# One more slot between the transposes of the values and those of the scaled key in each head pair's chain

## The chip, the cores and the metric

The kernel runs on one core of a Trainium2 chip. The metric is device time in microseconds (us) of one execution. Five engines work side by side, each through its own list of instructions and in the order of that list: PE (matmuls), DVE and ACT (elementwise work), POOL (elementwise work and the issue of some DMAs) and SP (the issue of the other DMAs). An engine whose next instruction waits, waits with everything that stands behind it.

## The reference

One layer of a hybrid encoder is computed for 1024 prompt frames and 64 sample frames, in fp32. A normalised input goes through one projection of 2560 columns, which are split among three token mixers; their outputs are normalised, joined, projected and added to the input, and a feed-forward part follows:

```python
proj = einsum('bld,de->ble', rmsnorm(x), w_in)
q, f_raw, inp, g, u, xr, gr = split(proj)
oA = hgrn2(q, f_raw, inp, g)   # 6 heads of 64: S = diag(f) S + k i^T, o = S^T q, norm, silu(g)
oB = s5(u)                     # 16 complex diagonal systems, 64 states each
oC = rglru(xr, gr)             # conv of width 4, two gates, h = a h + b, gelu(gr)
x = x + concat(oA, oB, oC) @ w_out
y = rmsnorm(x + (silu(rms(x) @ w_gate) * (rms(x) @ w_up)) @ w_down)
```

## The kernel before

The tokens are cut into three groups of 384, 384 and 320 (`GROUPS`). The first part of the program, some 550 us, holds the input projections, the three mixers and the output projection; the rest is the feed-forward part, which the change does not touch.

**Slots.** The input projection is done 128 columns at a time: `proj` issues 24 matmuls into one of two PSUM buffers of the tag "mm" and loads its two weight blocks, raw by SP, high part by ACT (L117), low part by ACT and a POOL DMA (L119, L120). After each projection `drive` calls `tick`, which lets every chain that is due take one step. One projection and the steps behind it are a *slot* here. PE takes its instructions strictly in the order in which the program issues them; DVE, ACT, POOL and SP are ordered by a scheduler by readiness and priority.

**Chains.** The 384 columns of a mixer are three head pairs. For each pair `inproj` does six projections in a row: xr, f, q, v, gr, g, each evacuated by DVE (L411, L425, L432, L437, L443, L453), which frees its "mm" buffer. With xr the chain `unit` of this pair starts, so there are nine chains, six slots apart, and one that lasts 15 slots overlaps the next two. A chain yields the number of slots to its next step: convolution (L490 to L492) at 0; the two gate matmuls (wab, wxb) at 2; logarithms (L511 to L521) at 3; exponentials at 4; the scaled queries and keys q32, Q2, k32, kh at 5; ks, in the tag "la" (L583 to L585), at 6; at 7 the transposes of v (`turned`, L604). Then come three steps which are each one slot behind the one before: kt, the transposes of ks, with the masked score matmuls (L618 to L658, called *masked* below); the state products kv and the state updates (L661 to L684); the output product po and its evacuation by ACT L696 and DVE L697. The square sums (sqn) follow two slots later.

**Shared storage.** All matmul results but the projections' share a ring of six PSUM banks, the tag "mx": masked takes four, the transposes and each gate one. The tag "d16" holds in turn l2 (L510, L512), d16, and the copy of kt; "la" holds the gate's la (L503) and then ks. There is one g per head pair in one buffer: L453 writes it, L697 reads it.

**The S5 mixer** has its own chain, which takes part in the same slots: scar/sbbr and scai/sbbi products, evacuated by ACT L899 and DVE L902 and written out by DMAs of SP (L909); transposes of sbv and sH, copied by DVE L888 into sMV; products with sMT, sMV and sX. After the last chain has started, `outproj(0)` does the output projection of the first group, with split operands mh (ACT L160) and ml (DVE L167).

Of the kernel before, what the change touches and what calls it, by code (L numbers as in the profile page):

```python
# [58 lines left out]
def trunk(ctx: ExitStack, tc: tile.TileContext, I: dict, O: list):  # L59
# [214 lines left out]
    with ExitStack() as ph1:  # L274
# [114 lines left out]
        def inproj(gi):  # L389
# [10 lines left out]
            for p in range(3):  # L400
                o = proj(gi, 1792 + 128 * p)
                with tc.high_priority(offset=WPRIO):
                    xr = tile_("xr", TMAX + 6)
                    off = 0
                    for s0, n, kind in grp["segs"]:
# [12 lines left out]
                        off += n + 3  # L418
                u = dict(xr=xr)
                spawn(unit(gi, p, u))  # L420
                yield
                o = proj(gi, 384 + 128 * p)
# [51 lines left out]
        def unit(gi, p, u):  # L474
# [116 lines left out]
            def turned(src, name, cp):  # L591
                dst = p1.tile([128, 3, 128], F32, tag=name, name="turned")
                pt = ps_mx()
                ptv = pt[:, :384].rearrange("p (c w) -> p c w", c=3)
                for c in range(ncp):
                    transpose(ptv[:tw[c], c, :], src(c), ident)
                nf = sum(1 for w in tw if w == 128)
                with soon():
                    cp(dst[:, :nf, :], ptv[:, :nf, :])
                    if nf < ncp:  # L600
                        cp(dst[:64, nf, :], ptv[:64, nf, :])
                return dst

            vt = turned(lambda c: u["v"][:, 128 * c:128 * c + tw[c]], "vt", A.copy)  # L604
            if p == 2:
# [8 lines left out]
                        stt(o, o, hc[:, 9 + j:10 + j], lsq[:, :T], op0=OP.mult, op1=OP.mult)  # L614

                pending.append((lsq[:, :T], 1.0 / (4 * DC), lru_done))
            yield 1
            kt = turned(lambda c: ks[:, 128 * c:128 * c + tw[c]], "d16", A.copy)  # L618
            a = am
            nf = sum(1 for w in tw if w == 128)  # L620
# [819 lines left out]
```

## Time and profile before

| what | value |
|---|---|
| time, median of 3 runs | 1385.76 us (1381.37 to 1386.45) |
| profiled execution | 1382.6 us, its span 1380.8 us |
| mean granted TensorE clock | 0.961 |
| PE busy | 1306.4 us, 95% of the span |
| DVE, ACT, POOL busy | 622.2, 634.5, 292.1 us |

The times of rows are counted from the start of the span. PE bounds the kernel as a whole; its idle time and its slower stretches lie almost wholly in the first 550 us, where DVE, ACT and SP each hold it up now and then.

### The profile page before, as it was taken

How to read it: one execution, taken by the hardware profiler on the slowest of the kernel's cores; microseconds unless marked ns; L12 is line 12 of the kernel's file. 1: busy time of each engine (PE TensorE's matmuls, PEld its weight loads, DVE VectorE, ACT ScalarE, POOL GpSimd, SP SyncE). 2: the span in 40 equal slices, each digit the busy share in tenths (PEclk: the TensorE clock that was granted, in tenths of full speed). 3: DMA queues.
4: the chain of work that ended last, by engine and by line, in shares of the span. 5: the costliest groups of instructions: out<-in, count | busy, mean ns of one | idle time of the engine just before them, and what ended most of it. 6: DMA issues, size and time to landing. Idle time of an engine off the chain costs nothing.

```text
span 1380.8 us, 21166 instructions
## 1 busy us (share of the span) xinstructions
PE 1306.4 (95%) x7872; PEld 1254.1 (91%) x7872; DVE 622.2 (45%) x1714; ACT 634.5 (46%) x1244; POOL 292.1 (21%) x359
## 2 busy tenths in 40 slices
PE   7886999999998999999999999999999999999995
PEld 6776798878887798999999999999999999999985
DVE  8884798857856677821121111221112111211287
ACT  7667566768976454542322332222321233222363
POOL 2233353444432000111122010220111111110000
PEclk8997899999988899999999999999999999999997
DMA  9967677768775245444355252553454335432343
GB/s 281 273 145 183 131 168 155 169 150 178 167 164 143 81 138 161 115 90 94 63 99 114 65 118 50 96 122 69 92 107 92 77 74 119 90 82 64 86 133 118
DMA packets 106119, 169.81 MB, mean 123 GB/s; under 512 B 12849, under 2 KB 35905, under 8 KB 106017
## 3 DMA queue, kind: packets, MB, share of 16 engines
q0 software_dynamic: 35936, 62.30, 28.2%
q1 hardware_dynamic: 70080, 106.16, 25.0%
q8 instruction: 62, 1.02, 0.3%
q14 instruction: 41, 0.33, 0.1%
HBM read 160.71 MB, written 7.12 MB: 122 GB/s over the span
## 4 chain that ended last, share of the span: by engine, by line
PE 51%; issue 25%; DVE 10%; POOL 6%; DMA 4%; ACT 3%; SPq 1%; POOLq 0%; DVEq 0%; ACTq 0%
PE pd L76 16%; PE pu L76 10%; PE pg L76 10%; PE mm L76 9%; PE mx L76 5%; POOL wlo L120 4%; DMA wlo<-in_w_in_dram 2%; DMA wlo<-in_w_up_dram 1%; ACT wlo L119 1%; ACT L138 1%; DMA xraw<-in_xT_dram 0%; ACT whi L117 0%; DMA raw<-in_w_in_dram 0%; DVE xl L328 0%; SPq L909 0%
## 5 line engine op out<-in xcount | busy, mean ns | idle before, releaser
L117 ACT CAST whi<-raw 128x512 fp32r<-128x512 f32 x320 | 190.2, 600 | 255.4 <-PE pd L76 175.3
L1332 DVE TENSOR_TENSOR sil<-pu,sil 128x384 f32<-128x384 f32 (+1 forms) x66 | 35.4, 536 | 398.9 <-PE pu L76 398.9
L76 PE MATMUL mm<-xh,whi 128*128 128x384 f32 (+1 forms) x480 | 170.0, 363 | 19.6 <-ACT whi L117 11.6
L76 PE MATMUL pd<-hh,whi 128*128 128x384 f32 (+1 forms) x528 | 172.2, 330 | 0.0
L76 PE MATMUL pd<-hl,whi 128*128 128x384 f32 (+1 forms) x528 | 171.5, 329 | 0.0
L76 PE MATMUL pg<-x2h,whi 128*128 128x384 f32 (+1 forms) x528 | 170.3, 327 | 0.6 <-ACT x2h L261 0.6
L76 PE MATMUL pg<-x2l,whi 128*128 128x384 f32 (+1 forms) x528 | 170.4, 327 | 0.3 <-DVE x2l L262 0.3
L76 PE MATMUL pu<-x2h,whi 128*128 128x384 f32 (+1 forms) x528 | 170.0, 326 | 0.0
L76 PE MATMUL pu<-x2l,whi 128*128 128x384 f32 (+1 forms) x528 | 169.9, 326 | 0.0
L76 PE MATMUL mm<-xl,whi 128*128 128x384 f32 (+1 forms) x480 | 158.4, 340 | 0.0
L119 ACT ACTIVATE wlo<-whi 128x512 fp32r<-128x512 f32 x248 | 145.1, 606 | 3.9 <-PE mm L76 0.9
L120 POOL DMA_DIRECT2D wlo<-in_w_in_dram x112 | 99.7, 974 | 215.3 <-ACT wlo L119 179.8
L1342 DVE TENSOR_TENSOR x<-pd,x 128x384 f32<-128x384 f32 (+1 forms) x120 | 64.3, 536 | 166.4 <-PE pd L76 166.2
L120 POOL DMA_DIRECT2D wlo<-in_w_gate_dram x44 | 42.6, 968 | 440.2 <-ACT wlo L119 433.8
L76 PEld LDWEIGHTS mm<-xh,whi 128*128 128x128 f32 x480 | 96.1, 202 | 28.2 <-ACT whi L117 13.3
L1333 ACT CAST hh<-sil 128x384 fp32r<-128x384 f32 (+1 forms) x66 | 32.7, 496 | 185.9 <-DVE sil L1332 185.9
L76 PE MATMUL pd<-hh,wlo 128*128 128x384 f32 (+1 forms) x528 | 107.5, 329 | 0.0
L76 PE MATMUL mm<-xh,wlo 128*128 128x384 f32 (+1 forms) x480 | 92.3, 332 | 9.3 <-DMA wlo<-in_w_in_dram 9.2
L76 PEld LDWEIGHTS pd<-hl,whi 128*128 128x128 f32 x528 | 100.3, 190 | 0.0
L76 PEld LDWEIGHTS pd<-hh,whi 128*128 128x128 f32 x528 | 100.2, 190 | 0.0
L76 PEld LDWEIGHTS pg<-x2l,whi 128*128 128x128 f32 x528 | 99.1, 188 | 1.0 <-DVE x2l L262 0.7
L76 PEld LDWEIGHTS pg<-x2h,whi 128*128 128x128 f32 x528 | 99.1, 188 | 0.9 <-ACT x2h L261 0.9
(428 smaller groups left out, 2525.8 us busy)
## 6 DMA issues: line engine op xcount, KB each, us to landing
raw<-in_w_in_dram SPq DMA_DIRECT2D x112, 256.0 KB, 4.5
wlo<-in_w_in_dram POOLq DMA_DIRECT2D x112, 256.0 KB, 5.9
raw<-in_w_down_dram SPq DMA_DIRECT2D x56, 256.0 KB, 2.7
raw<-in_w_out_dram SPq DMA_DIRECT2D x48, 256.0 KB, 3.0
raw<-in_w_gate_dram SPq DMA_DIRECT2D x44, 256.0 KB, 2.9
raw<-in_w_up_dram SPq DMA_DIRECT2D x44, 256.0 KB, 5.5
wlo<-in_w_gate_dram POOLq DMA_DIRECT2D x44, 256.0 KB, 4.7
wlo<-in_w_up_dram POOLq DMA_DIRECT2D x44, 256.0 KB, 6.6
```

The costliest lines, as they stand in the source:

```text
L76: in_order(PE.matmul(out, lhsT, rhs, start=start, stop=stop, **kw).ins)
L117: ins = A.copy(hi[:, :n, :], raw[:, :n, :]).ins
L119: A.activation(lo[:, :n, :], hi[:, :n, :].bitcast(F32), AF.Copy, scale=-1.0)
L120: G.dma_start(lo[:, :n, :], src[:, h0:h0 + n, :], accum_op=OP.add)
L138: ins = A.activation(out, in_, func, **kw).ins
L1332: tt(s_[:, :T], pu[:, :T], s_[:, :T], op=OP.mult)
L1333: A.copy(hh[:, t0:t0 + T], s_[:, :T])
L1342: tt(x1[gi][:, dm, :T], o[:, :T], x1[gi][:, dm, :T], op=OP.add)
```

## The change

One number: the chain waits two slots, not one, behind the transposes of v. kt with masked, kv, po and sqn come a slot later in each of the nine chains, and with them the chain's end. No instruction is added or taken away on any engine's arithmetic.

```diff
@@ unit(gi, p, u)
                 pending.append((lsq[:, :T], 1.0 / (4 * DC), lru_done))
-            yield 1
+            yield 2
             kt = turned(lambda c: ks[:, 128 * c:128 * c + tw[c]], "d16", A.copy)
```

On PE the first place is the slot at 154 us of the trace before, where the second chain is at its kt and the third at its gates. Before:

```order
L79 MATMUL mx<-ident,sbv 128x128 x2
L79 MATMUL mx<-ident,sH_1744 128x128 x2
L79 MATMUL mx<-ident,la 128x128 x3
L76 MATMUL mx<-qm,km 128x128 x6
...
L76 MATMUL mx<-xc,wab 128x384
L76 MATMUL mx<-xc,wxb 128x384
L76 MATMUL mm<-xh_342,whi 128x384
```

Now, with the projection of 24 matmuls and the S5 products in between left out:

```order
L79 MATMUL mx<-ident,sbv 128x128 x2
L79 MATMUL mx<-ident,sH_1741 128x128 x2
L76 MATMUL mx<-xc,wab 128x384
L76 MATMUL mx<-xc,wxb 128x384
L76 MATMUL mm<-xh_342,whi 128x384
...
L79 MATMUL mx<-ident,la 128x128 x3
L76 MATMUL mx<-qm,km 128x128 x6
```

The gates of the younger chain stay in their slot and go on right behind the transposes of S5; kt (ident,la) and masked (from qm,km on) stand behind the next projection.

On DVE the second place is the end of the third chain, at 230 to 237 us before: L697 is its output, L453 the g of the fourth chain. Before:

```order
L697 SCALAR_TENSOR_TENSOR mix0_714<-mx_2518,hc_493,g_2172 128x384 [waits Activation_49]
L614 SCALAR_TENSOR_TENSOR mix0_714<-mix0_714,hc_493,lsq_501 128x384 [waits Activation_49]
L614 SCALAR_TENSOR_TENSOR mix0_714<-mix0_714,hc_493,lsq_501 128x384 x2
L566 TENSOR_TENSOR dd_2748<-eb_2666 128x6x2 [waits Activation_49]
L569 TENSOR_TENSOR q32_2749<-q_2403,eb_2666 128x192
L567 TENSOR_TENSOR dd_2748<-dd_2748 128x6 [waits DVE_49]
L572 TENSOR_TENSOR Q2_2750<-q32_2749,eb_2666 128x6x2x16 [waits DVE_49]
L453 TENSOR_TENSOR g_2719<-mm_2694,rt1_92 128x384 [waits PE_49]
```

Now:

```order
L614 SCALAR_TENSOR_TENSOR mix0_714<-mix0_714,hc_493,lsq_501 128x384 [waits Activation_49]
L941 TENSOR_TENSOR sbv_2711<-st1_2603,mx_2714 128x2x137 [waits DVE_49]
L942 TENSOR_TENSOR sXb_2712<-st2_2604,mx_2713 128x2x137
L697 SCALAR_TENSOR_TENSOR mix0_714<-mx_2629,hc_493,g_2157 128x384 [waits Activation_49]
L943 TENSOR_TENSOR sX1_2710<-sbv_2711,sXb_2712 128x2x137 [waits DVE_49]
L453 TENSOR_TENSOR g_2704<-mm_2679,rt1_92 128x384 [waits DVE_49]
L614 SCALAR_TENSOR_TENSOR mix0_714<-mix0_714,hc_493,lsq_501 128x384 x2
```

L453 stands nearly at once behind L697, with a wait for DVE's own L697 in place of one for PE, since the old g is read a slot later than the new one is projected; the six instructions that stood between them come later.

## Rows read from the trace of the kernel before

**Rows 1.** Busy time by stretch: the densest of the mixers, and the feed-forward part.

```profile
core 0: us, PE busy (x) PEld busy (x) DVE busy (x) ACT busy (x) POOL busy (x), PEclk, DMA share, GB/s
180.00:240.00 60.00, 57.02 (x366) 51.63 (x363) 54.84 (x141) 37.79 (x77) 28.81 (x32) 0.97 0.78 165
540.00:1380.00 840.00, 820.38 (x4960) 815.62 (x4958) 221.88 (x483) 274.13 (x519) 117.22 (x136) 0.99 0.43 94
```

**Rows 2.** Waits of PE from 60 to 550 us: total, times, longest.

```profile
PE mm L76 <- DVE g L453: 4.1, 2, 3.0
```

**Rows 3.** Timeline of PE: start, length, instruction; the slot at 154, one like it.

```profile
154.21 0.49 PE L79 MATMUL mx<-ident,la 128*128 128x128 f32 x3
...
160.17 0.69 PE L76 MATMUL mx<-q,k 64*128 64x64 f32 x2 [3.32 <-DVE sMV L888]
...
171.13 0.39 PE L76 MATMUL mx<-scar,sbbr 64*16 64x128 f32 x2
...
204.33 0.49 PE L79 MATMUL mx<-ident,la 128*128 128x128 f32 x3
...
213.42 0.38 PE L79 MATMUL mx<-ident,sbv 128*128 128x128 f32 x2
```

**Rows 4.** Timeline of PE, two projections from 233 us, and two like them.

```profile
233.13 0.81 PE L76 MATMUL mx<-sqn,ones_h 128*128 128x384 f32 x2
236.91 0.69 PE L76 MATMUL mm<-xh,whi 128*128 128x384 f32 x1 [2.98 <-DVE g L453]
...
247.56 0.39 PE L76 MATMUL mx<-sU,sMT 128*128 128x137 f32 x2
...
280.71 0.91 PE L76 MATMUL mx<-sqn,ones_h 128*128 128x384 f32 x2
...
290.14 0.49 PE L79 MATMUL mx<-ident,la 128*128 128x128 f32 x3
```

**Rows 5.** Timeline of PE, the last products of two chains' po.

```profile
181.01 0.66 PE L76 MATMUL mx<-Q,hist 128*128 128x64 f32 x4
...
222.92 0.66 PE L76 MATMUL mx<-Q,hist 128*128 128x64 f32 x4
```

**Rows 6.** Timeline of DVE at the same two chains' ends.

```profile
186.23 0.60 DVE L697 SCALAR_TENSOR_TENSOR mix<-mx,hc,g 128x384 f32<-128x384 f32 x1
...
230.50 0.61 DVE L697 SCALAR_TENSOR_TENSOR mix<-mx,hc,g 128x384 f32<-128x384 f32 x1
231.03 3.23 DVE L614 SCALAR_TENSOR_TENSOR mix<-mix,hc,lsq 128x384 f32<-128x384 f32 x3
...
236.31 0.55 DVE L453 TENSOR_TENSOR g<-mm,rt 128x384 f32<-128x384 f32 x1
```

**Rows 7.** Timeline of PE behind the slot at 290 us.

```profile
295.20 1.65 PE L76 MATMUL mx<-xc,wab 128*128 128x384 f32 x2 [1.48 <-ACT turned L599]
298.58 1.65 PE L76 MATMUL mx<-xc,wxb 128*128 128x384 f32 x2 [1.73 <-ACT turned L599]
...
304.83 0.40 PE L76 MATMUL mx<-sU,sMT 128*128 128x137 f32 x2
```

**Rows 8.** Timeline of PE in the slot at 418 us.

```profile
418.33 0.52 PE L79 MATMUL mx<-ident,la 128*128 128x128 f32 x3 [2.64 <-DVE la L584]
...
427.34 1.41 PE L76 MATMUL mx<-xc,wab 128*128 128x320 f32 x2 [2.06 <-DVE xc L492]
...
433.91 0.93 PE L76 MATMUL mx<-turned 64*128 64x128 f32 x10
```

**Rows 9.** Timeline of PE at its longest wait.

```profile
95.14 1.04 PE L76 MATMUL mx<-qm,km 64*128 64x128 f32 x10
...
98.24 0.39 PE L76 MATMUL mx<-scar,sbbr 64*16 64x128 f32 x2
...
110.65 0.69 PE L76 MATMUL mm<-xh,whi 128*128 128x384 f32 x1 [9.43 <-ACT whi L117]
```

**Rows 10.** Waits of SP from 60 to 550 us.

```profile
SPq L909 <- DVE sysb L902: 22.7, 4, 11.3
```

**Rows 11.** Timeline of PE at the start of the output projection.

```profile
452.80 3.50 PE L76 MATMUL mm<-ml,whi 128*128 128x384 f32 x7 [2.58 <-DVE ml L167]
```

## The prediction

> **What bounds the kernel now.** I read the busy times by stretch first. In the feed-forward part PE is busy 820.4 of 840 us at a granted clock of 0.99 [rows 1]; the change moves nothing there. In the mixers PE still has the longest list, but DVE is nearly as full: between 180 and 240 us it is busy 54.8 of 60 us, PE 57.0 [rows 1]. So a wait of PE that is removed there is a gain only as far as DVE can follow; its 5.2 idle us in that stretch are the room. Second, the waits of PE and its timeline before 550 us. The reader is to see few and single waits with different causes, and that each costs more than its length, because the matmuls behind it run at the lower of the two clock levels (1.2 instead of 2.4 GHz) for a while. So each place is priced by comparing it with the same instructions elsewhere at full clock.
>
> **The change part by part.** Work is not added; kt, masked, kv, po and sqn of nine chains go one projection later. That costs or gains only where PE waits now, or would wait then.
>
> *The slot at 154 us.* kt to the start of the next slot's work takes 171.13 − 154.21 = 16.9 us; the same instructions, kt, masked, gates and a projection, take 213.42 − 204.33 = 9.1 us [rows 3]. So the place costs 7.8 us, 3.3 of them a wait and 4.5 slow clock. The wait is that of masked for a bank of the ring: DVE has copied sMV too late (L888). S5's two transposes, kt, four banks of masked and the gates, nine uses of six banks, fall into one slot. With the change masked stands behind the gates and a projection, some 6 us later on PE, and the copies' 3.3 us of lateness are covered. The DVE queue that made them late does not get shorter; it will then hold up a projection's buffer or a gate instead. Bounds 0 and −7.8; I take half, **−4**.
>
> *Two projections from 233 us.* sqn to the end of two projections takes 247.56 − 233.13 = 14.4 us, elsewhere 290.14 − 280.71 = 9.4 [rows 4]: 5.0 us lost, 3.0 of them a wait for DVE's L453, which must free the "mm" buffer. L453 comes at 236.31 although its product was long done: 3.2 us of L614, L566 and others stand between L697 and L453 [rows 6]. In the new order L453 is second behind L697, with most of these behind it. L697 itself waits for po, a slot later, but DVE reached it at 230.50, 6.9 us after po's last product ended (222.92 + 0.66) [rows 5, 6], so po can end one projection later, 4.3 us ((9.4 − 0.8) / 2, [rows 4]), before DVE notices. L453 would then come some 1.2 us behind L697, near 232, before the buffer is due at 233.9. Bounds +1 and −5.0; I take **−4**.
>
> *The slot at 290 us.* From kt at 290.14 to 304.83 are 14.7 us [rows 4, 7] against 9.1 [rows 3]: 5.6 lost. The gates wait for ACT's copy of kt, which stands in ACT's queue behind a weight block's high part; this came late because SP's queue had been held by L909. That wait, SP for L902, is the largest that S5 gives the DMA queue: four times, 22.7 us in all, 11.3 the longest [rows 10]. The gates no longer stand behind kt, but the next projection needs that same late weight block, and PE reaches it 3.6 us earlier, since kt and masked now come behind it. I expect most of the wait to move to the projection. Bounds +2 and −5.6; I take **−1.5**.
>
> *The first chain, 95 to 110 us.* This is the same cause before its longest wait, 9.4 us for a high part [rows 9]. Today masked, 98.24 − 95.14 = 3.1 us, and kt, 0.5, come ahead of the S5 products that start L902's chain; now these run 3.6 us sooner, and SP is released up to that much sooner, but 3.6 us of PE work move from ahead of the wait to behind it. The two cancel, except that a queue passes on less than it is given. Bounds 0 and +3.6; I take **+1**.
>
> *The slot at 418 us.* From the end of a projection at 418.33 − 2.64 = 415.69 to 433.91 pass 18.2 us, for work that takes at most 9.1 [rows 8, 3]. kt waits 2.64 us for L584, then the gates 2.06 us for the convolution, L492, whose steps on DVE were interleaved with masked's evacuation. Now kt has a slot's cover and its wait goes; but the gates come straight behind the projection, where the convolution is not ready either. The two waits and the 7 us of slow kt and masked between them end at 427.34; without masked's evacuations in between, the convolution should be done about 5.5 us behind the projection, so one wait of about 5.5 us takes the place of two of 4.7. What is won is some slow clock: bounds +2 and −9.1; nearest is the wait that stays, so **−2**.
>
> *The start of the output projection.* The first ml (L167) is 2.6 us late and is followed by seven matmuls in 3.5 us, about twice the length at full clock [rows 11]. The last chains are a slot longer now, so DVE has more of them at this time, and ml stands in the same queue. Bounds 0 and +6; I take **+2**.
>
> *The new wait.* L453 of chains 2 to 9 waits for L697, so for po in the same slot. Behind po lies one projection, 4.3 us, until the buffer is due; L696, L697 and L453 need about 1.6 (L697 and L453 0.6 each [rows 6], L696 taken as the same). So it waits only if DVE is more than 2.7 us behind. At 186 us DVE is 4.6 us behind po (186.23 − 181.67), at 230 us 6.9 [rows 5, 6]. Because po itself comes later while DVE's backlog does not, most of that is used up. Bounds 0 and +10; I take **+1**. Nothing but the DVE instructions behind L453 is queued behind this wait, and these serve the next chain's steps.
>
> *What DVE gives back.* 8 us are to be gained at 154 and 233 us, both around a stretch with 5.2 us of DVE idle. I charge **+2** (bounds 0 and +5).
>
> Sum: −4 − 4 − 1.5 + 1 − 2 + 2 + 1 + 2 = **−5.5 us**. The profiled execution took 1382.6 us, 1.8 of them outside its span of 1380.8; 5.5 less gives 1377.1. The median of the runs, 1385.76, lies 3.2 above the profiled one, so a median would be 1380.3. I forecast **1380 us**.
>
> The Trainium skill, in "TensorE: Matmul & The Clock Gate", section "A second HAM failure mode: psum-queue depth-cycling", says that short idle moments of PE between groups of matmuls, while results cycle through PSUM banks, can make its clock fall and rise again and again. The rows agree in kind: 3.3 us of wait at 160.17 go with 4.5 us of slow matmuls [rows 3]. By that rule a change that replaces one long wait with several short ones would gain nothing, and the sum by it would be about 0; without the rule the sum stays −5.5.
>
> **The rivals.** *Nothing to measure.* All gains are taken back: DVE and SP release the same buffers at the same times, and PE only waits elsewhere. For it speaks DVE's 54.8 of 60 us [rows 1] and that two of the five places hang on SP and the weight blocks, not on the order of PE. Against it: at 154 us the banks, not the queue, were short. It gives −2 to +2, so about 1386 on the median.
>
> *Slower, by the buffers of the projections.* L453 behind L697 holds one of only two "mm" buffers through po, L696 and L697 at eight places, from the slot of the second chain's g on. If DVE's backlog is as far behind the later po as it was behind the earlier, the projection two slots on waits 4.6 − 2.7 = 1.9 us at the place of 186 us and 6.9 − 2.7 = 4.2 us at that of 230 us [rows 5, 6], each with slow matmuls behind, as long again by [rows 3]: some 12 us. With what is won at 154 us it gives +8, 1394 on the median. The point from which it decides: L697 starting more than 2.7 us behind po's last product. Against it: today PE waits only twice for L453, 4.1 us in all [rows 2], though the same queue stands ahead of it.
> The Trainium skill ("Perfetto Trace Analysis", section "Optimization Strategy") reads a gap that repeats on the engine that should be busy as a sign that too few buffers are there for the next tile. Today's rows show two such waits of nine [rows 2], so they do not bear it out yet; with it, all eight places would repeat the gap.
>
> *All of it.* The places at 154, 233 and 290 us lose their full 7.8, 5.0 and 5.6 us and DVE gives nothing back: with the other terms as above, −18.4 − 2 + 1 + 2 + 1 = −16.4 us, 1369 on the median. For it: these are waits for single late instructions, and DVE has idle time at other moments. Against it: the third hangs on SP.
>
> **How the numbers follow.** Forecast, −1 to −10: 0.42. Nothing: 0.20. Slower: 0.20. All of it: 0.18. About 0.5%, 6.9 us, is what a measurement of this kernel can tell from no change. A bit over a third of the forecast case lies beyond −6.9, 0.16, and all of the large case: faster 0.34. Slower by over 0.5%: nearly all of its case, 0.18. The rest, 0.48, is within. The range goes from the large case to somewhat beyond +6.9: 1369 to 1393. The likeliest case alone is 1376 to 1385.
>
> **What would show it.** Right, if masked in the slot of 154 us no longer waits for L888, if no projection behind 233 us waits for L453, and if one longer wait for the convolution stands near 416 us. Wrong, if the waits for L453 grow to more than the 4.1 us of today, if the wait for the high part at 110 us grows by more than 3.6 us, or if the waits for ml add up to more than 8 us. The clock of the mixers' part must rise with the gain; if it does not, the waits have only moved.

## The result: slower by 0.8%, and the profile after

The changed kernel takes 1395.26 us (median of 13 runs, 1390.59 to 1401.6), the kernel before 1385.31 beside it (13 runs, 1376.15 to 1392.15): a ratio of 1.0083, 95% interval 1.006 to 1.0105. Forecast were 1380 us, and a range of 1369 to 1393. The profiled execution took 1395.05 us, its span 1393.3, 12.5 more than before. The number of instructions on each engine is the same; they wait more.

Where the time went is read at points at which both kernels have issued the same matmuls. The starts of the next matmul there, in us, from one profiled execution of each:

| matmuls issued | before | after | after − before | step | forecast for the step |
|---|---|---|---|---|---|
| 377 | 90.49 | 89.65 | −0.84 | | |
| 661 | 149.53 | 152.41 | +2.88 | +3.7 | first chain +1 |
| 772 | 172.55 | 167.68 | −4.87 | −7.8 | slot at 154 us −4 |
| 872 | 185.75 | 181.14 | −4.61 | +0.3 | none |
| 951 | 199.87 | 202.95 | +3.08 | +7.7 | none |
| 1215 | 242.82 | 242.03 | −0.79 | −3.9 | projections from 233 us −4 |
| 1503 | 285.89 | 293.11 | +7.22 | +8.0 | none |
| 1765 | 333.01 | 342.11 | +9.10 | +1.9 | slot at 290 us −1.5 |
| 2013 | 372.95 | 380.57 | +7.62 | −1.5 | none |
| 2239 | 410.39 | 417.94 | +7.55 | −0.1 | none |
| 2882, `pd<-mh`, output projection | 535.27 | 547.62 | +12.35 | +4.8 | slot at 418 −2, output projection +2 |

The feed-forward part begins at 568.82 us before and at 579.94 after, and from there to the end pass 812.0 and 813.4 us. So nearly all is lost in the mixers. There the table shows gains and losses of up to 8 us, not one cost that repeats. A step of 2 us or less says little: the kernel `not_last_group` below has the same PE order up to its last three chains, and its steps up to 1765 matmuls differ from these by up to 2.2 us.

The busy time by stretch after the change: the two stretches of [rows 1], the whole of the mixers, and two stretches to which the text comes back below:

```profile
core 0: us, PE busy (x) PEld busy (x) DVE busy (x) ACT busy (x) POOL busy (x), PEclk, DMA share, GB/s
60.00:540.00 480.00, 432.42 (x2604) 388.05 (x2605) 341.87 (x879) 315.62 (x635) 158.23 (x180) 0.91 0.66 151
158.00:172.00 14.00, 14.00 (x105) 12.77 (x103) 7.73 (x25) 10.85 (x24) 3.50 (x4) 1.00 0.88 186
180.00:240.00 60.00, 56.30 (x344) 50.39 (x344) 50.50 (x135) 38.18 (x75) 25.04 (x28) 0.91 0.71 151
190.00:203.00 13.00, 9.33 (x30) 6.57 (x30) 9.27 (x36) 4.64 (x10) 5.27 (x6) 0.69 0.81 164
540.00:1380.00 840.00, 828.57 (x5012) 823.98 (x5010) 223.06 (x475) 278.38 (x527) 117.07 (x136) 0.99 0.43 94
```

Between 180 and 240 us, where DVE was full before, it is now busy 50.50 us in place of 54.84, and the granted clock is 0.91 in place of 0.97. DVE has fewer instructions done there (135, not 141) and PE 344 instead of 366. Both engines do less in the same time than before.

Waits of PE after the change, from 60 to 560 us (total, times, longest), to be read beside [rows 2]:

```profile
PE mx L76 <- DVE xc L492: 14.3, 3, 9.0
PE mm L76 <- ACT whi L117: 8.8, 1, 8.8
PE mx L76 <- POOL sX L958: 4.5, 3, 2.3
PE mm L76 <- DVE ml L167: 4.0, 2, 3.6
...
PE mm L76 <- DVE hlast L540: 3.0, 1, 3.0
PE mx L76 <- DVE sX L955: 2.6, 2, 1.6
PE mx L76 <- DVE lsq L580: 2.4, 1, 2.4
PE mm L76 <- DVE g L453: 2.0, 2, 1.3
```

The waits at which the change aimed are gone: L888 (3.3 us before), kt's copy L599 (3.2) and L584 (2.6) do not appear. In their place stand waits that were not there: for S5's sX (L955 and L958, 7.1 us together), for lsq (L580), and more for the convolution (L492, 7.6 us before). All of these are results of late DVE or POOL work, and none is made by a step that the change moves.

The waits for L453 have grown, not shrunk. 2.0 us stand under its own name, 4.1 before. But the 3.0 us put down to L540 are its as well: L540 copies one column of the scan's result, which no projection needs. The projection that starts at 330.25 needs the buffer that L453 frees, and DVE has L453 in front of L540, behind L697 and the scan L537:

```profile
326.66 0.62 DVE L697 SCALAR_TENSOR_TENSOR mix<-mx,hc,g 128x384 f32<-128x384 f32 x1
327.20 2.45 DVE L537 TENSOR_TENSOR_SCAN lr<-la,hlast,xc 128x384 f32<-128x384 f32 x1
329.57 0.53 DVE L453 TENSOR_TENSOR g<-mm,rt 128x384 f32<-128x384 f32 x1
```

So L453 holds PE up for 5.0 us in all. (In `not_last_group`, with the same PE order there, this one wait is absent.)

The timeline of PE after, at the places of [rows 3, 7, 8, 9, 11]:

```profile
105.73 0.69 PE L76 MATMUL mm<-xh,whi 128*128 128x384 f32 x1 [8.76 <-ACT whi L117]
...
164.11 0.55 PE L79 MATMUL mx<-ident,la 128*128 128x128 f32 x3
...
191.58 0.50 PE L76 MATMUL mx<-sX,scar 64*128 64x137 f32 x2 [1.61 <-DVE sX L955]
194.16 0.50 PE L76 MATMUL mx<-sX,scai 64*128 64x137 f32 x2 [2.09 <-POOL sX L958]
...
287.95 0.41 PE L76 MATMUL mm<-xh,whi 128*128 128x384 f32 x1 [0.67 <-DVE g L453]
...
330.25 0.38 PE L76 MATMUL mm<-xh,whi 128*128 128x320 f32 x1 [2.98 <-DVE hlast L540]
...
338.95 0.88 PE L76 MATMUL mx<-lsq,ones 128*128 128x384 f32 x2 [2.44 <-DVE lsq L580]
...
430.73 1.41 PE L76 MATMUL mx<-xc,wab 128*128 128x320 f32 x2 [9.01 <-DVE xc L492]
...
465.01 3.50 PE L76 MATMUL mm<-ml,whi 128*128 128x384 f32 x7 [3.55 <-DVE ml L167]
```

At 772 matmuls both kernels have the slot at 154 us behind them, kt and masked included. From 661 matmuls to there it took 23.02 us before and takes 15.27 after: 7.75 us are won, the whole of the bound of 7.8, and the clock is 1.00 from 158 to 172 us, where it was 0.63 before. At 872 matmuls PE is still 4.6 us ahead. It reaches S5's products with sX at 189.97 (191.58 − 1.61), and there it stops: from 872 to 951 matmuls pass 21.81 us, against 14.12 before, with 3.7 us of waits and the clock at 0.69 between 190 and 203 us. So 7.7 us are lost in one place. The same wait comes again at 247 and 250 us (1.0 and 2.3 us).

Why is sX not ready? DVE after the change, from 172 us on:

```profile
172.18 0.56 DVE L443 TENSOR_TENSOR gr<-mm,rt 128x384 f32<-128x384 f32 x1 [3.71 <-PE mm L76]
...
176.03 0.96 DVE L520 TENSOR_TENSOR_SCAN G<-sm,d 128x384 f32<-128x384 bf16 x1
...
182.34 0.62 DVE L697 SCALAR_TENSOR_TENSOR mix<-mx,hc,g 128x384 f32<-128x384 f32 x1
...
183.34 0.55 DVE L453 TENSOR_TENSOR g<-mm,rt 128x384 f32<-128x384 f32 x1
...
187.92 2.19 DVE L950 TENSOR_TENSOR_SCAN sH<-sD,sX 128x276 f32<-128x276 f32 x2
...
191.09 0.43 DVE L955 TENSOR_TENSOR sX<-sbv,sXb 128x276 f32<-128x276 f32 x1
```

DVE sits idle for 3.71 us up to 172.18, and from then on has the updates of kv (L679), the next chain's scan (L520) and the differences for its exponentials, L697 with the new L453, and then S5's scans (L950). L955 comes at 191.09; before, it came at 192.33. PE has moved 4.6 us forward, sX only 1.2.

The scan L520 is late because of ACT. The next chain's logarithms on ACT, of the kernel before (tanh of its gates as `lr<-mx`, L503 as `la<-lr`, L512 as `d<-f,small`):

```profile
164.61 0.58 ACT L138 ACTIVATE lr<-mx,hc 128x384 f32<-128x384 f32 x1 [0.71 <-PE mx L76]
165.22 0.71 ACT L138 ACTIVATE la<-lr,sp 128x384 f32<-128x384 f32 x1
...
174.33 0.60 ACT L138 ACTIVATE d<-f,small 128x384 f32<-128x384 f32 x1
```

The same after the change:

```profile
158.56 0.58 ACT L138 ACTIVATE lr<-mx,hc 128x384 f32<-128x384 f32 x1
...
165.38 0.46 ACT L599 COPY turned<-mx 128x384 f32<-128x384 f32 x1
165.75 0.70 ACT L138 ACTIVATE la<-lr,sp 128x384 f32<-128x384 f32 x1
...
174.17 0.62 ACT L138 ACTIVATE d<-f,small 128x384 f32<-128x384 f32 x1 [0.46 <-PE mx L76]
```

The gates come 6 us earlier, but `la` no longer follows its tanh at once: it stands behind kt's copy (L599), a slot later. From tanh to L512 pass 15.6 us (174.17 − 158.56), before 9.7. The reason is in the storage. ks (L583) and the gate's `la` (L503) have the tag "la", kt's copy and L512's result the tag "d16", one buffer each. The new `la` may be written only when kt's transposes have read ks, and L512 only when kv's products have read kt. One more slot ahead of kt holds both buffers a slot longer, and the next chain's first steps on ACT and DVE wait there. The trace bears this out chain by chain: after the change, in each of the eight chains that follow another, `la` starts within 1.3 us of the end of the transposes of ks, and L512 within 1.0 us of the end of kv's last product. What the sharing costs is tested in the second set of experiments.

### The profile page after: what moved, and what is told of

Read it like the earlier page. It is cut to its first block, busy times and chain, and to the rows that moved or that the text cites. A ratio compares the mean times of both kernels' runs of the same rounds, so it can differ in the third digit from the quotient of the medians.

```text
span 1393.3 us, 21171 instructions
## 1 busy us (share of the span) xinstructions
PE 1313.5 (94%) x7872; PEld 1259.0 (90%) x7872; DVE 623.7 (45%) x1714; ACT 636.5 (46%) x1244; POOL 293.4 (21%) x359
## 4 chain that ended last, share of the span: by engine, by line
PE 61%; issue 16%; DVE 10%; DMA 5%; POOL 5%; ACT 2%; SPq 1%; POOLq 0%; DVEq 0%; ACTq 0%
PE pd L76 19%; PE pg L76 14%; PE pu L76 14%; PE mm L76 9%; PE mx L76 5%; POOL wlo L120 3%; DMA xraw<-in_xT_dram 1%; DMA wlo<-in_w_up_dram 1%; DMA raw<-in_w_in_dram 1%; DVE hist L679 1%; DMA yd<-sysb 1%; DVE lr L537 1%; PE pt L76 1%; DVE mix L1065 1%; DMA wlo<-in_w_in_dram 0%
## 5 line engine op out<-in xcount | busy, mean ns | idle before, releaser
L76 PE MATMUL mm<-xl,whi 128*128 128x384 f32 (+1 forms) x480 | 161.3, 345 | 0.9 <-DVE xl L328 0.9
L76 PEld LDWEIGHTS mm<-xh,whi 128*128 128x128 f32 x480 | 96.1, 201 | 28.2 <-ACT whi L117 15.4
L76 PEld LDWEIGHTS mm<-xl,whi 128*128 128x128 f32 x480 | 96.8, 203 | 4.2 <-DVE xl L328 2.0
```

What stands on the lines that cost most here:

```text
L76: in_order(PE.matmul(out, lhsT, rhs, start=start, stop=stop, **kw).ins)
```

## Experiments

Each was timed beside the kernel before on the same chip; before had medians of 1380.94, 1381.57 and 1381.59 us in the three sets. The third set ran on another chip than the first two. The edits are to the changed kernel unless said otherwise; all ratios are to the kernel before.

**The first set: the order on DVE, g's buffer, the last group.** Theory A was that S5's scans only stand too far behind in DVE's queue, rival B that the rule "L453 behind L697" holds the projections' buffers, rival C that the loss arises in the last chains.

`s5_first_after` and `s5_first_before` (the same edit on the kernel before):

```diff
-            for i, nm in ((0, "sr"), (1, "si")):
+            with soon():
+                for i, nm in ((0, "sr"), (1, "si")):
...
```

(L945 to L958 inside, with no other change.)

> The changed kernel, with the scans and products of S5 that end in sX (L945 to L958) given priority on DVE and POOL. Theory A: the change is slower because the kv updates and L697 of each chain, now a slot later, stand ahead of S5's scans in DVE's queue, so that PE waits for sX in the slots at 191 and 248 us (6.97 us in all) and then runs at the lower clock; with the scans ahead the waits for sX fall under 1 us and the kernel comes to 0.2 to 0.6% above the one before, 8 us under the changed one at the most. Rival B (the projection buffer that L453 frees late): no wait of it is touched, the time stays 0.6 to 1.0% above. Rival C (the last chains: the wait for xc at 430 us and for ml): stays as well, 0.6 to 1.0% above.

> The kernel before with the same priority for S5's scans, as the control: PE waits nowhere for sX there. Theory A: within 0.3% of the kernel before, since there is no wait to win. If it gains as much as the changed kernel does, the priority is a gain by itself and says nothing on the change.

Measured: 1390.45 us, 1.0056 (1.0037 to 1.0075), and for the control 1377.15 us, 0.9966 (0.9951 to 0.9981). Waits of PE in the first:

```profile
PE mx L76 <- DVE xc L492: 18.2, 4, 8.8
...
PE mx L76 <- DVE hist L679: 5.2, 3, 2.3
```

The waits for sX are gone and the time lies in A's range, at its upper end. But PE now waits for kv's updates (L679) and longer for the convolution, and the 0.27% by which the medians differ from the changed kernel (the intervals overlap) are won on the kernel before as well, 0.34%, more than A allowed there. By what was put on record this says nothing on the change: A is neither shown nor refuted here. It does show that most of the loss stays when sX is no longer late.

`g_in_mix_after`:

```diff
-                    g = u["g"] = tile_("g")
+                    g = u["g"] = mix[gi][:, p, :]
```

> The changed kernel with g kept in the place of its result in mix, so that L453 has no older g to wait for. Rival B (the wait of L453 for L697, which holds a projection buffer): the order of DVE goes back to L453 right behind its product, the waits of PE for L453 and those shown as L540 at 330 us go, and 5 to 8 us are won: 0.2 to 0.5% above the kernel before. Theory A and rival C: at most 2 us are won, 0.6 to 1.0% above.

Measured: 1399.87 us, 1.0123 (1.0101 to 1.0145). Here L453 needs no buffer of its own and can come as soon as its projection is done. Waits of PE:

```profile
PE mx L76 <- DVE lsq L580: 7.6, 1, 7.6
PE mx L76 <- DVE sX L955: 4.6, 2, 3.2
...
PE mm L76 <- DVE mix L453: 1.1, 1, 1.1
```

Of the waits for L453 one of 1.1 us is left, the one shown as L540 is gone, and the kernel is no faster: 0.4% slower by the medians, with intervals that just overlap, and outside every range that was expected. B falls: the late L453 is there, but to free it wins nothing.

`not_last_group`:

```diff
-            yield 2
+            yield 1 if gi == 2 else 2
```

> The added slot only in the chains of the first two groups; the last three chains as before. Rival C (loss in the last chains and at the start of the output projection): the wait for xc of 9.0 us goes back to 2 to 4.7 and that for ml to 2.6, 4 to 6 us are won, 0.4 to 0.5% above the kernel before. Theory A: the losses in the first two groups stay, 0.4 to 0.9% above. If it comes out at the kernel before or under it, all of the loss is in the last group.

Measured: 1390.1 us, 1.006 (1.0042 to 1.0078). By the medians the last group carries about 0.23 of the 0.83%, though the intervals overlap. The wait of 9.0 us for the convolution becomes 2.1, as C expected, and one of 5.0 for L584 comes instead. C falls: most of the loss needs the slot in the first two groups.

**The second set: the storage (theory D).** D says that the buffers that ks and kt share with the next chain make its logarithms late. Both are given others, which already exist and which the next chain writes only from its exponentials on, a slot behind kt:

```diff
-            ks = tmp("la")
+            ks = tmp("ee")
...
-            kt = turned(lambda c: ks[:, 128 * c:128 * c + tw[c]], "d16", A.copy)
+            kt = turned(lambda c: ks[:, 128 * c:128 * c + tw[c]], "eb", A.copy)
```

`own_space_after` has both, `own_space_before` both on the kernel before (without the added slot), `kt_space_after` and `ks_space_after` one line each.

> The changed kernel with ks in the storage of ee and kt's copy in that of eb, so that neither the next chain's la (L503) nor its l2 (L512) waits for them. Theory D: the added slot lets kt's copy hold d16, and ks hold la, a slot longer; the next chain's logarithms then start only behind kv, DVE idles in the slot of the gates (4.3 us of 6.3 at 168 us) and gets the work of two steps in the next ones, so PE waits for sX, lsq and xc later on. With storage of their own DVE's idle time there falls under 3 us, the wait for lsq at 339 us goes, and at least 8 of the 11.5 us come back: 0.0 to 0.25% above the kernel before, or under it. Theory A' (the kv updates themselves, 12 a chain, come into a full slot, whatever the logarithms do): no more than 3 us come back, 0.6 to 1.0% above.

> The kernel before with the same storage, as the control. Theory D: there l2 waits for kv in the same slot only, so at most 3 us are won: 0.2% under to 0.1% above the kernel before. If it wins as much as the changed kernel does, the shared storage is a cost of both and does not explain the difference.

> The changed kernel with only kt's copy moved to eb's storage; ks stays in that of la. Theory D, if l2 is the one that counts: most of what both give, 0.1 to 0.4% above the kernel before. If la counts: little, 0.6 to 1.0% above. Theory A': 0.6 to 1.0% above.

> The changed kernel with only ks moved to ee's storage; kt's copy stays in that of d16. Theory D, if l2 is the one that counts: little, 0.6 to 1.0% above the kernel before. If la counts: 0.1 to 0.4% above. Theory A': 0.6 to 1.0% above.

| | shared | only ks apart | only kt apart | both apart |
|---|---|---|---|---|
| before | 1 | | | 0.9974 (0.996 to 0.9987) |
| with the slot added | 1.0083 | 1.0049 (1.0031 to 1.0067) | 1.0014 (0.9999 to 1.0029) | **0.9943** (0.9923 to 0.9963), 1373.26 us |

With the added slot the two lines are worth 1.4%, without it 0.26%, a little more than the 0.2% that D allowed. So what the added slot costs is the sharing. With the storage apart, the slot gains: 0.9943 / 0.9974 = 0.9969, about 4.8 us (1378.02 − 1373.26; the two intervals overlap by 0.0003, so the sign is likely and the size rough).

The two lines singly give back 0.34 and 0.69%, together 1.40. ACT's part of the reason is in the traces. Medians over the chains of the third to the ninth head pair, in us behind the start of the tanh:

| kernel | to `la` (L503) | to L512 |
|---|---|---|
| before | 0.9 | 7.1 |
| with the slot added | 5.7 | 15.3 |
| with the slot, only ks apart | 0.6 | 15.4 |
| with the slot, only kt apart | 6.0 | 14.0 |
| with the slot, both apart | 0.6 | 7.5 |
| before, both apart | 0.9 | 6.7 |

With ks alone apart, L512 still waits for kv. With kt alone apart, L512 still stands in ACT's queue behind an `la` that waits for ks. Only both edits bring L512 back. Why kt alone is worth 0.69% although L512 comes hardly sooner is not shown.

ACT in `own_space_after`, to be read beside the two excerpts above:

```profile
161.14 0.57 ACT L138 ACTIVATE lr<-mx,hc 128x384 f32<-128x384 f32 x1
161.74 0.71 ACT L138 ACTIVATE la<-lr,sp 128x384 f32<-128x384 f32 x1
...
168.64 0.61 ACT L138 ACTIVATE d<-f,small 128x384 f32<-128x384 f32 x1
```

And DVE:

```profile
170.37 0.96 DVE L520 TENSOR_TENSOR_SCAN G<-sm,d 128x384 f32<-128x384 bf16 x1 [0.62 <-POOL d L516]
...
174.99 1.64 DVE L537 TENSOR_TENSOR_SCAN lr<-la,hlast,xc 128x384 f32<-128x384 f32 x1
...
185.70 1.70 DVE L950 TENSOR_TENSOR_SCAN sH<-sD,sX 128x276 f32<-128x276 f32 x2
...
189.01 0.44 DVE L955 TENSOR_TENSOR sX<-sbv,sXb 128x276 f32<-128x276 f32 x1
```

`la` follows its tanh at once again, and tanh to L512 is 7.5 us. The scans L520 and L537 now come before the evacuation of the gr projection (L443), ahead of which DVE was idle for 3.71 us in the changed kernel; L537 stood at 186.81 there, shortly before L950. S5's L955 comes 2.1 us earlier. PE's waits:

```profile
PE mm L76 <- ACT whi L117: 13.1, 1, 13.1
PE mx L76 <- DVE xc L492: 8.1, 3, 3.9
...
PE mm L76 <- DVE g L453: 3.1, 2, 2.0
```

No sX, no lsq, no ml. `pd<-mh` starts at 525.00 us, 10.3 ahead of the kernel before, although the first wait for a high part is the longest of all (13.1; it is 13.4 with the storage apart and no slot) and 661 matmuls are reached only at 155.16 us, 5.6 later than before. The mixers' stretch of this kernel:

```profile
60.00:540.00 480.00, 445.07 (x2740) 404.59 (x2740) 356.22 (x919) 323.59 (x654) 156.31 (x179) 0.94 0.66 157
```

The granted clock is 0.94 here, 0.91 after the change, and PE issues 2740 matmuls in the 480 us instead of 2604.

**The third set: does anything of A or B, or the first chain, come back once the storage is apart?** All four are made on `own_space_after`, with the edits above; `own_space_not_first` has

```diff
-            yield 2
+            yield 1 if gi == p == 0 else 2
```

> The changed kernel with storage of their own for ks and kt's copy, and S5's scans first as well. Theory D: with the storage apart PE has no wait for sX left, so the priority wins at most 2 us more: 0.4 to 0.75% under the kernel before. Theory A (S5's place in DVE's queue is a cause of its own): 4 us or more on top, 0.8% under or better.

> The changed kernel with storage of their own for ks and kt's copy, and g kept in mix, so that L453 waits for no older g. Rival B in the form left to it (with the storage apart L453 behind L697 is what remains; PE waits 3.1 us for g): 2 to 4 us more, 0.7 to 0.9% under the kernel before. If the late L453 costs nothing, within 1.5 us of the kernel without it: 0.45 to 0.7% under; if it was right that g in mix does harm, as in the changed kernel, 0.2% under or worse.

> The changed kernel with storage of their own for ks and kt's copy, and the first of the nine chains without the added slot. The first chain's term: masked of this chain comes behind the longest wait (13.1 us for a high part at 110 us) in place of ahead of it; if that costs the 3 to 4 us by which PE falls back there against the kernel before with the same storage, it is 0.75 to 0.95% under the kernel before; if the wait only grows by what is taken out, 0.45 to 0.65% under.

> The same with S5's scans first as well: all that seems to win at once. Theory D and the first chain's term together: 0.8 to 1.1% under the kernel before; if neither adds to the storage, 0.45 to 0.7% under.

| kernel | us | ratio to before |
|---|---|---|
| own_space_s5_first | 1378.15 | 0.9977 (0.9963 to 0.9991) |
| own_space_g_in_mix | 1377.71 | 0.9977 (0.9959 to 0.9994) |
| own_space_not_first | **1370.67** | 0.9933 (0.9911 to 0.9955) |
| own_space_not_first_s5_first | 1375.96 | 0.9966 (0.9951 to 0.9982) |

With S5 first the ratio is now 0.34% higher (0.9977 against 0.9943; the intervals touch), and 0.33% higher without the first chain's slot, where it had won 0.34% on the kernel before. That is outside what D expected and the reverse of what A wanted: A falls here. Freeing g costs 0.34% by the medians here too, with intervals that overlap. Leaving out the first chain gives the lowest median, but 0.9933 and 0.9943 can't be told apart, so the first chain's slot costs nothing that could be measured; the two edits together came out slower than either range expected.

## Why the prediction was wrong, point by point

The step that failed stands at the head of the part by part: "Work is not added", and a move "costs or gains only where PE waits now, or would wait then". The prediction then looked for waits at PE's own places and for one new wait on DVE (L453). A step that is moved also holds its operands longer, and these lie in buffers that another chain's work needs. That work is on ACT and DVE, not on PE, so no place at which PE waited before shows it. The kernel's text told it: both tags stand in the part on the kernel above. The prediction took no term from them.

- *The slot at 154 us, −4.* Right that the wait for L888 goes. The gain up to 772 matmuls is 7.75 us, the whole of the bound. It was given back at sX, 7.7 us. "DVE gives back +2 (0 to +5)" was the term for this, and too small: its size was taken from DVE's 5.2 idle us, but what happened is that DVE stood idle ahead of its backlog, 3.71 us in one piece. Together the two make +0.2 up to 951 matmuls: one wait of 3.3 us gave way to two of 1.6 and 2.1. With storage apart the waits for sX are absent.
- *Two projections from 233 us, −4.* Right in size: −3.9, and neither of the two projections waits. L697 and L453 came at 234.94 and 235.82 rather than near 232, and the buffer was still not due.
- *From 242 to 286 us.* No term; +8.0 measured. Here stands the second wait for sX with its slow clock.
- *The slot at 290 us, −1.5.* The gates no longer wait for kt's copy, but the step to 1765 matmuls is +1.9, with the new wait of 3.0 us for L453 at 330 us. Inside the bound of +2.
- *The first chain, +1 (0 to +3.6).* +3.7 measured. The wait for the high part is 8.8 us, not longer than before [rows 9], and ends 4.9 us sooner (105.73 against 110.65), more than the 3.6 us of work that moved; so it is not shown that "a queue passes on less than it is given". SP's waits for L902 are 20.5 us in all against 22.7 [rows 10]. Up to 484 matmuls, at 122 us, the step is +1.3; the rest comes behind it, by 139 us, where the clock is 0.86 in place of 0.92. In `own_space_after` the same step is +7.3, and the kernel is faster all the same; leaving it out changes nothing that can be measured. So a loss up to 150 us is no measure of the end.
- *The slot at 418 us, −2, and the output projection, +2.* Right in kind: L584's wait goes and one for the convolution takes the place of two. It is 9.0 us, not 5.5. ml's is 3.55 instead of 2.58. Together +4.8. What was late is xr, the convolution's input: its one buffer (`tile_("xr")`) serves the chain before as scratch up to L580, and DVE came to L580 late, behind S5's output norm (L1065) and the scaled queries and keys (L566 to L573):

```profile
420.40 4.36 DVE L1065 SCALAR_TENSOR_TENSOR mix<-ys,hc,sq 128x96 f32<-128x96 f32 x8 [0.58 <-ACT sq L138]
...
426.93 0.48 DVE L580 TENSOR_TENSOR lsq<-lsq,xr 128x320 f32<-128x320 f32 x1
...
427.64 0.41 DVE L411 TENSOR_TENSOR xr<-mm,rt 128x256 f32<-128x256 f32 x1
```

  In `own_space_after` L580 comes at 411.50, 1.6 us behind the point of 2239 matmuls instead of 9.0; the convolution's wait is 3.25 us, there is none for ml, the clock of the step is 0.96 instead of 0.88, and against before the step is −9.8. Of the 22.6 us by which `own_space_after` is ahead of the changed kernel at 2882 matmuls, 14.6 arise here.
- *The new wait, L453 behind L697, +1.* It came, once: L453's waits are 5.0 us with the one at 330 us, against 4.1 [rows 2], which the prediction had named as a sign that it is wrong. The rival that was slower rested on this; its +8 is near the measured +10, but its mechanism carries little of it: freeing g takes these waits away and the kernel is no faster. It was given 0.20, and its time was right by accident.

The forecast gain is near in its sum alone: with the shared storage out of the way, the slot is worth about −4.8 us, where −5.5 was summed. Place by place it is not the forecast's gain, and that the sums agree is luck. The slot at 154 us takes 15.3 us in `own_space_before` as well as in `own_space_after`: the storage by itself takes the wait for L888 away, and nothing is left there for the slot to win. The projections from 233 us gain 0.3 us, not 4. What the slot wins with the storage apart, by the profiled executions, stands behind 2239 matmuls: 11.7 us, where the forecast had 0; up to there it loses 3.0. (These two executions differ by 11.1 us, the medians by 4.8; the one of `own_space_before` was its slowest.)

What was missing is the term that `own_space_after` against the changed kernel measures: 1.0083 − 0.9943, 1.4% or some 19 us, of which 0.26% is there without the slot too. So some 16 us (1.14%) come with the slot, and these turn −4.8 into the measured loss.

The Trainium skill's reading of repeating gaps ("Perfetto Trace Analysis", section "Optimization Strategy"), that they can mean too few buffers for the next tile, was weighed for the "mm" buffers and does not hold for them here. Too few buffers was the cause, but of two other tiles. Their delay repeats in every chain on ACT, which waited for the buffers; the gaps that it left on PE did not repeat.

What stays open: why freeing g costs 0.3 to 0.4% by the medians, with the storage shared and apart, and why the first chain loses behind its long wait. Moving po a slot also puts its reading of Q2 into the slot in which the next chain writes Q2; no run gave Q2 a buffer of its own. Edits that only let DVE's work come earlier, S5 first or g in mix, move this kernel by 0.3 to 0.4% either way, about as much as the slot gains with the storage apart; the 1.4% of the two storage lines is well beyond that.

## What to carry to other kernels

When a step of a software-pipelined chain is moved later, list for each of its operands the buffer and who writes that buffer next: a buffer shared between a chain's late step and the next chain's early step turns a free slot into a delay of the next chain. Such a delay shows on the engine that writes (here ACT, an activation that no longer follows its predecessor) and not on the one that bounds; look there for a step whose distance from its own input has grown. Test it by giving the tile another buffer on both orders: if the edit is worth much more on the new order (1.4% against 0.26%), the sharing was the price.

## What the runs showed of the hardware

A wait costs more than its length by the clock: the 79 matmuls from the 872nd on, the products with sX among them, took 7.7 us more for waits of 3.7 us, with a granted clock of 0.69 from 190 to 203 us (part of the time at 1.2, part at 2.4 GHz). From 158 to 172 us it had been 1.00.

The same hint of order, S5 first, changed the time by −0.34% on the kernel before and by +0.34% on `own_space_after` (there the intervals touch). What an order on one queue is worth was not carried over from one version of this kernel to the next.
